# Low parts of the first weight pieces ordered behind the powers of the first norm, and reciprocals of row sums on 16 columns between two turns by 32x32 blocks

## The chip, the cores and the metric

The kernel runs on one core of a Trainium2 chip. The metric is the device time of one execution in microseconds (us), as the median of several runs. A core has five instruction queues that run beside each other and meet through semaphores: TensorE (PE in the rows, with its weight loads as PEld), VectorE (DVE), ScalarE (ACT), GpSimd (POOL) and SyncE (SP), from which the transfers (DMA) of this kernel are issued.

## The reference

One sequence of 512 tokens with 1024 channels goes through two blocks. The first block has three branches on one normed input, which are gated and merged; the second runs twice and has two attentions and an MLP.

```python
def rms_norm(x, g):
    y = xf * lax.rsqrt(jnp.mean(xf * xf, axis=-1, keepdims=True) + EPS)
    return (y * g).astype(x.dtype)

def first_block(...):
    h = rms_norm(x, g_norm)
    q, k, v, fl, gf, u, gs, qm, gm, gl = split_cols(h @ w_in)
    log_f = log_sigmoid(fl + b_forget)
    y_fox = forgetting_attention(q, k, v, log_f) * silu(gf)   # 12 heads of 64, causal softmax
    y_s5 = gelu(s5_ssm(u, ...))                               # diagonal complex scan
    y_s5 = y_s5 * sigmoid(y_s5 @ w_glu + b_glu) * silu(gs)
    y_mem = memory_attention(qm, mk, mv) * silu(gm)           # 4 heads, 256 memory tokens
    merged = sum of sigmoid(gl + b_merge) * (y_branch @ w_proj_branch)
    return rms_norm(x + merged @ w_out, g_final)

def second_block(x, c, ...):
    for l in range(2):
        h = rms(x, g_mix[l]) * (1 + sc1) + sh1                # sh, sc, gt from silu(c) @ w_ada
        y_a = gqa_attention(...) @ w_branch_a[l]              # 8 query heads, 2 key heads
        y_b = dilated_attention(...) @ w_branch_b[l]          # 3 groups of 4 heads, joined by their sums
        x = x + gt1 * ((gate_a * y_a + gate_b * y_b) @ w_out[l])
        x = x + gt2 * (square(relu(h2 @ w_ff1[l])) @ w_ff2[l])
```

Each softmax divides by the sum of its row; the change touches how the kernel forms the reciprocal of these sums, and the order of the work in the first `rms_norm`.

## The kernel before

**Layout and products.** Activations lie with channels on the 128 partitions and the 512 tokens along the columns. A float32 product is made of three matmuls on parts: each operand is split into a high part (rounded to fp32r) and a low part (the value less its high part), and PE adds high by high, high by low and low by high. Weights come in pieces of 512 KB by DMA into three buffers `wr`. `split` (L81) makes two tiles of each: the high part `wh` by a cast on ACT (L93), the low part `wl` by a subtraction (L96), on POOL for every second piece (`WP = 2`) and on DVE for the others. `get` (L105) hands out a piece; `ahead` splits the next three and fetches three more. For activations the high part is L229 or L231 on ACT (`h`), the low part L237 or L239 on DVE (`l`).

**The first norm.** It is done in two halves of 256 tokens. For one half, ACT squares each 128 channels (L186 for the first, L190 for the others, into `sq`), DVE adds them up (L191, `sacc`), PE sums over the partitions (L197, `ps`), DVE turns the sums into mean plus epsilon (L215, `nv`), POOL raises it to the power −0.5 (L217, `nr`), PE spreads the result over the partitions (L204), DVE multiplies x with it and the gain (L568, `hu`), ACT and DVE split it, and PE runs the first products: L600 and L601 take the high part of the activations with both parts of the weights, L606 the low part. In `head`, `stat(0)` and `stat(1)` issue the first half's and the second half's chain up to the spread. With `begun` false, which holds for the first block alone, `head` takes its three pieces by `get` between `stat(0)` and the first products, and calls `ahead` for the next three after the first half's high products (L603).

**The softmax units.** A unit covers two heads. DVE takes row maxima (L352, `unm`), PE forms scores (L327, `ps`), ACT exponentiates (L395, `pe`) and casts (L397, `ph`), DVE forms the low part (L399, `pl`), and PE multiplies with the values, to which columns of ones are joined, so that the product holds the row sums beside the output (L416 to L418, `ppv`). `out_item` ends a head: ACT copies the 64 rows of sums to one half of `rs` (L443) and the output to one half of `y` (L444). Every one of the 64 rows holds the same sum for its token. After the second head of a pair, DVE takes the reciprocal of the whole `rs` (L446), and POOL multiplies (L447). This happens 18 times: 6 in the first block and 6 in each layer of the second.

**What sets the order.** All tiles of 512 columns come from one ring of 73 buffers. The order of the instructions on each engine is found when the program is built, by a scheduler that plays a timeline of its own; a dependency of the kind `AFTER` holds in this order alone and leaves no wait in the program. The S5 branch is issued in small steps between the attention's items (`tick`): its scans (`s5g`, L1324), its mixed weights (`s5bw`) and, later, its low parts `yl` (L1128). In the second block keys and queries are normed and split in L652 to L726 (`xg`, `qk`, `kl`), and powers of small tiles are carried to PE through bfloat16 parts (L274 to L284, `mcq`).

Of the kernel before, what the change touches and what calls it, by code (L numbers as in the profile page):

```python
# [9 lines left out]
F32 = mybir.dt.float32  # L10
# [4 lines left out]
ALU = mybir.AluOpType  # L15
# [8 lines left out]
def f32(t):  # L24
    return t.bitcast(F32)


class Core:
    def __init__(self, ctx, tc, a):
        self.ctx, self.tc, self.nc, self.a = ctx, tc, tc.nc, a  # L30
        self.n = 0
        self.base = ctx.enter_context(tc.tile_pool(name="base", bufs=1))
        self.psx = ExitStack()
        self.psum({"mm": 3, "s": 4, "=a": "s", "pv": 1, "=m": "s"})
        self.wp = ctx.enter_context(tc.tile_pool(name="wp", bufs=1))
        self.ring = ctx.enter_context(tc.tile_pool(name="ring", bufs=1))
        self.strips = []
        self.iw = 0
        self.raw, self.hl, self.cur = {}, {}, {}
        self.bg = []  # L40
        self.sums = {}
        self.pe = None

    AFTER = mybir.DependencyInfo(mybir.DependencyClass.NoSync, mybir.DependencyReason.SCHED_ONLY)
    NU = 73
# [35 lines left out]
    def split(self, i):  # L81
        if i >= len(self.strips) or i in self.hl:
            return
        self.fetch(i)
        n = self.strips[i][1].shape[-1]
        r = self.raw.pop(i)
        self.raw[i] = None
        eng = self.nc.gpsimd if i % self.WP == self.WP - 1 else self.nc.vector
        self.hl[i] = []
        for c in range(0, n, T):  # L90
            m = min(T, n - c)
            h, l = self.u(F32R, "wh"), self.u(F32R, "wl")
            ins = self.nc.scalar.copy(h[:, 0:m], r[:, c:c + m])  # L93
            if self.pe is not None:
                self.tc.add_manual_dep(ins.ins, self.pe, self.AFTER, reason="weights")
            eng.tensor_tensor(out=l[:, 0:m], in0=r[:, c:c + m], in1=f32(h)[:, 0:m], op=ALU.subtract)  # L96
            self.hl[i].append((h, l))

    def ahead(self, i):
# [108 lines left out]
    def rstd(self, sacc, cols):  # L208

        nc = self.nc  # L210
        nb = len(cols)
        pq = self.p("m")
        self.sumcols(pq, sacc, cols)
        v = self.t(self.base, [128, 4], F32, "nv", 2)[:, 0:nb]
        nc.vector.tensor_scalar(out=v, in0=pq[:, 0:nb], scalar1=1.0 / D, scalar2=1e-6, op0=ALU.mult, op1=ALU.add)  # L215
        r = self.t(self.base, [128, 4], F32, "nr", 2)[:, 0:nb]
        nc.gpsimd.tensor_tensor(out=r, in0=v, in1=self.mhalf[:, 0:nb], op=ALU.pow)  # L217
        return self.bcast(r)

    def hsplit(self, src, bias=None, out=None):  # L220
# [6 lines left out]
    def hi(self, src, bias, out):  # L227
        if bias is None:
            self.nc.scalar.copy(out[0], src)  # L229
        else:  # L230
            self.nc.scalar.activation(out=out[0], in_=src, func=AF.Identity, bias=bias)  # L231

    def lo(self, src, bias, out):
        nc = self.nc
        h, l = out
        if bias is None:
            nc.vector.tensor_tensor(out=l, in0=src, in1=f32(h), op=ALU.subtract)  # L237
        else:
            nc.vector.scalar_tensor_tensor(out=l, in0=src, scalar=bias, in1=f32(h), op0=ALU.add, op1=ALU.subtract)  # L239


class Att(Core):
# [44 lines left out]
    def rows(self, mc, tag, psum_tag, out=None):  # L287

        nc = self.nc
        pt = self.turn(mc, psum_tag)  # L290
        if out is None:
            out = self.t(self.base, [128, T], BF16, tag, 2)
            nc.scalar.copy(out, pt)
        else:
            nc.scalar.copy(out[96:128], pt[96:128])
        return out

    def unit(self, nh, sregs, tregs, qk, vsl, dst, extra=None, nq=4, hd=64, orow=None, fold=None):

# [4 lines left out]
        nc = self.nc  # L304
# [99 lines left out]
        def pv_item(j, i):  # L404
            ph, pl, pvs = st.pop(("p", j, i))
            pv = st["pv", j]
            mm = nc.tensor.matmul
            for x, (g, kb, c) in enumerate(pvs):
                vh, vl = vsl(j, g, kb)
                o = c  # L410
                f = i == 0 and x == 0
                z = i == nt - 1 and x == len(pvs) - 1
                if not isinstance(c, slice):
                    o = slice(0, 4 * (c[1] - c[0]))
                h, lo = self.like(ph[:, o], c), self.like(pl[:, o], c)
                mm(self.cut(pv, c), vh, h, start=f, stop=False)  # L416
                mm(self.cut(pv, c), vl, h, start=False, stop=False)  # L417
                mm(self.cut(pv, c), vh, lo, start=False, stop=z)  # L418
            if i == nt - 1:
                out_item(j)  # L420

        def vrow(j):

            if own_sum:
                return slice(0, 128)
            o = 64 * (j % 2) if orow is None else orow(j)
            return slice(o, o + 64)

        def out_item(j):
            pv = st.pop(("pv", j))  # L430
            v = vrow(j)
            if own_sum:
                rb = self.u(name="rb")
                pb = self.p("m")
                nc.tensor.matmul(pb, self.selr1[j], st["mr"], start=True, stop=True)
                nc.scalar.copy(rb, pb)
                nc.vector.tensor_tensor(out=dst(j), in0=pv, in1=rb, op=ALU.mult)
                return
            if j % 2 == 0:
                st["rs"] = self.u(name="rs")  # L440
            rows = slice(64 * (j % 2), 64 * (j % 2) + 64)
            rs, y = st["rs"], dst(j)
            nc.scalar.copy(rs[rows], pv[64 - v.start:128 - v.start])  # L443
            nc.scalar.copy(y[rows], pv[v])  # L444
            if j % 2 == 1:
                nc.vector.reciprocal(out=rs, in_=rs)  # L446
                nc.gpsimd.tensor_tensor(out=y, in0=y, in1=rs, op=ALU.mult)  # L447

        s = [(lambda j=j, q=q: s_item(j, q)) for j in range(nh) for q in range(nq)]
# [35 lines left out]
class Blk2(Att):  # L485
# [93 lines left out]
    def head(self, names, h, posts, norm, view, byw=False, begun=False):  # L579

        pms = [self.p("mm" if i else "pv") for i in range(len(names))]
        stat, hi, lo = norm
        if not begun:
            stat(0)
        ws = [self.get(n, 8, begun) for n in names]
        if not begun:
            hi(0)
        stat(1)
        lo(0)
        for hf in range(2):  # L590
            if hf == 1:
                hi(1)
                lo(1)
            ah, al = [[view(t, hf) for t in ts] for ts in h]
            mm = self.nc.tensor.matmul
            wo = list(zip(ws, (view(pm, hf) for pm in pms)))
            for g in [[v] for v in wo] if byw else [wo]:
                for k in range(8):
                    for w, o in g:
                        mm(o, w[k][0], ah[k], start=k == 0, stop=False)  # L600
                        self.pe = mm(o, w[k][1], ah[k], start=False, stop=False).ins.name  # L601
                if hf == 0 and not begun:
                    self.ahead(self.iw)  # L603
                for k in range(8):
                    for w, o in g:
                        self.pe = mm(o, w[k][0], al[k], start=False, stop=k == 7).ins.name  # L606
        for pm, post in zip(pms, posts):
            self.done(pm, post)
            self.tick()
# [1511 lines left out]
```

## Time and profile before

| what | value |
|---|---|
| median of 3 runs | 2417.26 us (2416.67 to 2422.07) |
| the profiled execution's own time | 2420.52 us |
| its span in the trace | 2418.5 us |
| mean granted TensorE clock | 0.984 |
| TensorE busy | 2310.7 us, 96% |
| VectorE busy | 1508.5 us, 62% |
| ScalarE busy | 1055.8 us, 44% |
| GpSimd busy | 875.4 us, 36% |
| reciprocals of `rs` (L446) | 18, 60.2 us |

The page is made from one execution. Its span runs from the first to the last instruction in the trace; the execution's own time has some 2 us around it. A busy share is an average over the whole span. An engine's instruction has a start, a duration and, where the engine stood idle before it, the length of that idle time and what ended it. The chain that ended last is followed back from the end, each step to what released it.

### The profile page before, as it was taken

Reading aid. Unit: us, or ns where it says so; the run is one execution under the profiler, and the core shown is the slowest. Engines: PE = TensorE matmul, PEld = TensorE weight load, DVE = VectorE, ACT = ScalarE, POOL = GpSimd, SP = SyncE. Lnnn points to the kernel's source line nnn. Section 1 sums busy time; section 2 is a strip of 40 time slices with the busy share of each in tenths; the row PEclk is TensorE's granted clock in tenths of the full one; section 3 lists DMA queues with packets and bytes.
Section 4 is the critical chain, followed back from the end, with each engine's and each line's share of the span. In section 5 each row is a group of like instructions: output and inputs, shape, how many; then the busy total and the mean of one; then the engine's idle time right before and its main releaser. Section 6 shows DMA issues by size and latency. Waiting matters only on the chain.

```text
span 2418.5 us, 32948 instructions
## 1 busy us (share of the span) xinstructions
PE 2310.7 (96%) x12071; PEld 1933.5 (80%) x12098; DVE 1508.5 (62%) x2467; ACT 1055.8 (44%) x1973; POOL 875.4 (36%) x722
## 2 busy tenths in 40 slices
PE   6999999998999899999999999999899999999999
PEld 5877777877788877788888888888778888888888
DVE  6666778666899788657378673257864746422222
ACT  4354553453333436653444324334565433523432
POOL 2443556733232284235132223126521713222212
PEclk9999999999999999999999999999999999999999
DMA  5211122313576331122247563242211314223322
GB/s 171 78 44 53 44 84 95 118 49 115 207 258 247 117 107 52 53 83 85 68 132 260 199 219 122 79 140 75 79 44 51 116 53 140 75 94 111 100 84 87
DMA packets 105617, 265.37 MB, mean 110 GB/s; under 512 B 13664, under 2 KB 23408, under 8 KB 105456
## 3 DMA queue, kind: packets, MB, share of 16 engines
q1 hardware_dynamic: 104304, 261.50, 32.2%
q8 instruction: 95, 1.56, 0.3%
q10 hardware_dynamic: 1152, 1.77, 0.2%
q14 instruction: 66, 0.54, 0.1%
HBM read 244.72 MB, written 9.44 MB: 105 GB/s over the span
## 4 chain that ended last, share of the span: by engine, by line
PE 75%; DVE 11%; issue 5%; POOL 4%; ACT 3%; DMA 2%; SPq 0%; ACTq 0%; another core or an unknown queue 0%; POOLq 0%; DVEq 0%
PE pmm L124 19%; PE pmm L126 19%; PE pmm L125 19%; PE ps L327 5%; PE ppv L416 1%; PE ppv L418 1%; PE pmm L141 1%; PE ppv L417 1%; PE pmm L142 1%; PE pmm L140 1%; DVE wl L96 1%; DVE l L239 1%; ACT wh L93 1%; POOL wl L96 1%; DVE adacc L521 1%
## 5 line engine op out<-in xcount | busy, mean ns | idle before, releaser
L96 POOL TENSOR_TENSOR wl<-wr,wh 128x512 fp32r<-128x512 f32 x346 | 489.6, 1434 | 1160.3 <-ACT wh L93 1037.2
L126 PE MATMUL pmm<-h,wl 128*128 128x512 f32 (+1 forms) x2104 | 823.4, 392 | 9.0 <-POOL wl L96 5.3
L124 PE MATMUL pmm<-h,wh 128*128 128x512 f32 (+1 forms) x2104 | 823.3, 392 | 7.2 <-ACT wh L93 4.3
L125 PE MATMUL pmm<-l,wh 128*128 128x512 f32 (+1 forms) x2104 | 819.7, 390 | 0.0
L126 PEld LDWEIGHTS pmm<-h,wl 128*128 128x128 f32 x2104 | 399.6, 190 | 94.3 <-POOL wl L96 7.7
L124 PEld LDWEIGHTS pmm<-h,wh 128*128 128x128 f32 x2104 | 399.8, 190 | 86.2 <-ACT wh L93 5.6
L125 PEld LDWEIGHTS pmm<-l,wh 128*128 128x128 f32 x2104 | 399.6, 190 | 78.4 <-DVE l L237 0.8
L93 ACT CAST wh<-wr 128x512 fp32r<-128x512 f32 (+1 forms) x692 | 387.5, 612 | 146.3 <-DMA wr<-in_w 85.9
L96 DVE TENSOR_TENSOR wl<-wr,wh 128x512 fp32r<-128x512 f32 x346 | 276.2, 827 | 39.3 <-ACT wh L93 34.6
L399 DVE TENSOR_TENSOR pl<-pe,ph 128x512 fp32r<-128x512 f32 (+4 forms) x168 | 113.6, 689 | 132.1 <-ACT ph L397 131.1
L237 DVE TENSOR_TENSOR l<-r,h 128x512 fp32r<-128x512 f32 x64 | 46.6, 728 | 221.3 <-ACT h L229 216.5
L1010 DVE SCALAR_TENSOR_TENSOR x<-pmm,ada,x 128x512 f32<-128x512 f32 (+1 forms) x88 | 60.0, 682 | 178.7 <-PE pmm L126 178.3
L521 DVE SCALAR_TENSOR_TENSOR adacc<-adw,cact,adacc 128x512 f32<-128x512 f32 x168 | 154.4, 921 | 4.1 <-DMA adw<-in_wada 0.9
L327 PE MATMUL ps<-qk,qk 128*128 128x512 f32 (+4 forms) x416 | 140.8, 366 | 12.6 <-DVE unm L352 8.6
L1033 ACT ACTIVATE r<-pmm 128x512 f32<-128x512 f32 x62 | 37.1, 598 | 246.0 <-PE pmm L126 246.0
L395 ACT ACTIVATE pe<-ps 128x512 f32<-128x512 f32 (+4 forms) x168 | 84.5, 503 | 114.7 <-PE ps L327 113.3
L327 PEld LDWEIGHTS ps<-qk,qk 128*128 128x128 f32 x416 | 79.3, 192 | 29.4 <-DVE unm L352 12.4
L124 PE MATMUL pmm<-yh,wh 128*128 128x512 f32 (+1 forms) x244 | 90.4, 374 | 5.8 <-ACT yh L1466 3.8
L125 PE MATMUL pmm<-yl,wh 128*128 128x512 f32 (+1 forms) x244 | 90.4, 371 | 2.7 <-DVE yl L1128 2.7
L397 ACT CAST ph<-pe 128x512 fp32r<-128x512 f32 (+4 forms) x168 | 89.1, 530 | 6.5 <-ACT pe L395 0.4
L126 PE MATMUL pmm<-yh,wl 128*128 128x512 f32 (+1 forms) x244 | 89.5, 369 | 0.0
L352 DVE TENSOR_REDUCE unm<-ps 128x1 f32<-128x512 f32 (+2 forms) x112 | 65.1, 597 | 25.6 <-PE ps L327 25.3
(393 smaller groups left out, 3925.0 us busy)
## 6 DMA issues: line engine op xcount, KB each, us to landing
wr<-in_w SPq DMA_DIRECT2D x324, 512.0 KB
adw<-in_wada SPq DMA_DIRECT2D x192, 256.0 KB
xs<-xg SPq DMA_DIRECT2D x136, 64.0 KB
wr<-in_w SPq DMA_DIRECT2D x22, 384.0 KB
xd<-x SPq DMA_DIRECT2D x16, 256.0 KB
x<-xd SPq DMA_DIRECT2D x16, 256.0 KB
x<-in_x SPq DMA_DIRECT2D x16, 128.0 KB
x<-in_x SPq DMA_DIRECT2D x8, 256.0 KB
```

Source lines behind the costliest of these rows:

```text
L93: ins = self.nc.scalar.copy(h[:, 0:m], r[:, c:c + m])
L96: eng.tensor_tensor(out=l[:, 0:m], in0=r[:, c:c + m], in1=f32(h)[:, 0:m], op=ALU.subtract)
L124: mm(out, wh, ah, start=start, stop=False)
L125: mm(out, wh, al, start=False, stop=False)
L126: self.pe = mm(out, wl, ah, start=False, stop=stop).ins.name
L327: mm(outs[i] if len(r.shape) == 2 else outs[i].rearrange("p (r i) -> p r i", r=r.shape[1]), w, r, start=first and i == 0, stop=last and i ...
L352: nc.vector.tensor_reduce(out=nm, in_=pts[0], axis=AX.X, op=ALU.max, negate=True)
L395: nc.scalar.activation(out=e[:, w], in_=pt[:, w], func=AF.Exp)
L397: nc.scalar.copy(ph[:, w], e[:, w])
L399: nc.vector.tensor_tensor(out=pl[:, w], in0=e[:, w], in1=f32(ph)[:, w], op=ALU.subtract)
L521: nc.vector.scalar_tensor_tensor(out=acc, in0=w, scalar=cc, in1=acc, op0=ALU.mult, op1=ALU.add)
L1010: nc.vector.scalar_tensor_tensor(out=x[j][:, s], in0=pm[:, s], scalar=ada[:, c + j:c + j + 1], in1=x[j][:, s], op0=ALU.mult, op1=ALU.add)
```

## The change

There are two edits, independent of each other.

*The low parts of the first pieces.* `power` keeps the name of the last power instruction. In `head`, for the first norm alone, the low parts of its three pieces are ordered behind the first half's power, and those of the three pieces of `ahead` behind the second half's power, by the same kind of dependency, which holds in the order alone.

*The reciprocals.* `inv_rows` turns `rs` by blocks of 32x32 on DVE into a new ring tile `rt`, so that the 32 partitions of a block, all with the same sum for a token, become 32 equal columns and the tokens lie along partitions; takes the reciprocal of the first column of each of the 16 blocks (128x16); and turns it back, reading each of these columns 32 times.

```diff
--- before.py
+++ after.py
@@ -40,6 +40,7 @@
         self.bg = []
         self.sums = {}
         self.pe = None
+        self.lo_after = None
 
     AFTER = mybir.DependencyInfo(mybir.DependencyClass.NoSync, mybir.DependencyReason.SCHED_ONLY)
     NU = 73
@@ -93,7 +94,9 @@
             ins = self.nc.scalar.copy(h[:, 0:m], r[:, c:c + m])
             if self.pe is not None:
                 self.tc.add_manual_dep(ins.ins, self.pe, self.AFTER, reason="weights")
-            eng.tensor_tensor(out=l[:, 0:m], in0=r[:, c:c + m], in1=f32(h)[:, 0:m], op=ALU.subtract)
+            ins = eng.tensor_tensor(out=l[:, 0:m], in0=r[:, c:c + m], in1=f32(h)[:, 0:m], op=ALU.subtract)
+            if self.lo_after is not None:
+                self.tc.add_manual_dep(ins.ins, self.lo_after, self.AFTER, reason="behind the power")
             self.hl[i].append((h, l))
 
     def ahead(self, i):
@@ -214,7 +217,7 @@
         v = self.t(self.base, [128, 4], F32, "nv", 2)[:, 0:nb]
         nc.vector.tensor_scalar(out=v, in0=pq[:, 0:nb], scalar1=1.0 / D, scalar2=1e-6, op0=ALU.mult, op1=ALU.add)
         r = self.t(self.base, [128, 4], F32, "nr", 2)[:, 0:nb]
-        nc.gpsimd.tensor_tensor(out=r, in0=v, in1=self.mhalf[:, 0:nb], op=ALU.pow)
+        self.power = nc.gpsimd.tensor_tensor(out=r, in0=v, in1=self.mhalf[:, 0:nb], op=ALU.pow).ins.name
         return self.bcast(r)
 
     def hsplit(self, src, bias=None, out=None):
@@ -294,6 +297,16 @@
         else:
             nc.scalar.copy(out[96:128], pt[96:128])
         return out
+
+    def inv_rows(self, rs):
+
+
+        nc = self.nc
+        rt = self.u(name="rt")
+        nc.vector.transpose(out=rt, in_=rs)
+        ri = self.t(self.base, [128, 16], F32, "ri", 2)
+        nc.vector.reciprocal(out=ri, in_=rt.rearrange("p (b c) -> p b c", c=32)[:, :, 0])
+        nc.vector.transpose(out=rs.rearrange("p (b c) -> p b c", c=32), in_=ri.unsqueeze(2).to_broadcast([128, 16, 32]))
 
     def unit(self, nh, sregs, tregs, qk, vsl, dst, extra=None, nq=4, hd=64, orow=None, fold=None):
 
@@ -443,7 +456,7 @@
             nc.scalar.copy(rs[rows], pv[64 - v.start:128 - v.start])
             nc.scalar.copy(y[rows], pv[v])
             if j % 2 == 1:
-                nc.vector.reciprocal(out=rs, in_=rs)
+                self.inv_rows(rs)
                 nc.gpsimd.tensor_tensor(out=y, in0=y, in1=rs, op=ALU.mult)
 
         s = [(lambda j=j, q=q: s_item(j, q)) for j in range(nh) for q in range(nq)]
@@ -582,6 +595,7 @@
         stat, hi, lo = norm
         if not begun:
             stat(0)
+            self.lo_after = self.power
         ws = [self.get(n, 8, begun) for n in names]
         if not begun:
             hi(0)
@@ -600,7 +614,9 @@
                         mm(o, w[k][0], ah[k], start=k == 0, stop=False)
                         self.pe = mm(o, w[k][1], ah[k], start=False, stop=False).ins.name
                 if hf == 0 and not begun:
+                    self.lo_after = self.power
                     self.ahead(self.iw)
+                    self.lo_after = None
                 for k in range(8):
                     for w, o in g:
                         self.pe = mm(o, w[k][0], al[k], start=False, stop=k == 7).ins.name
```

The first place is POOL's order at the first norm. `nr_204` and `nr_290` are the powers of the two halves, `wl` the low parts; `wl_220` and `wl_224` belong to the second of the first three pieces, the other four to two of the next three. Before:

```order
L96 ISA
L96 TENSOR_TENSOR wl_220<-wr_145,wh_219 128x512
L96 TENSOR_TENSOR wl_224<-wr_145,wh_223 128x512
L217 TENSOR_TENSOR nr_204<-nv_202,mhalf_72 128x2
L96 TENSOR_TENSOR wl_352<-wr_217,wh_351 128x512
L96 TENSOR_TENSOR wl_356<-wr_217,wh_355 128x512
L96 TENSOR_TENSOR wl_368<-wr_237,wh_367 128x512
L96 TENSOR_TENSOR wl_372<-wr_237,wh_371 128x512
L217 TENSOR_TENSOR nr_290<-nv_288,mhalf_72 128x2
```

The same place after the change:

```order
L220 ISA
L220 TENSOR_TENSOR nr_204<-nv_202,mhalf_72 128x2
L97 TENSOR_TENSOR wl_220<-wr_145,wh_219 128x512
L97 TENSOR_TENSOR wl_224<-wr_145,wh_223 128x512
L220 TENSOR_TENSOR nr_290<-nv_288,mhalf_72 128x2
L97 TENSOR_TENSOR wl_352<-wr_217,wh_351 128x512
L97 TENSOR_TENSOR wl_356<-wr_217,wh_355 128x512
L97 TENSOR_TENSOR wl_368<-wr_237,wh_367 128x512
L97 TENSOR_TENSOR wl_372<-wr_237,wh_371 128x512
```

Each power has moved ahead of the low parts that stood before it. On DVE the first half's low parts stand behind `nv_202` in the same way, four of them still ahead of the first `hu`.

The second place is DVE's order in the second half, from the second of its squares' sums (`sacc_176`) to the first `hu`. Before:

```order
L191 TENSOR_TENSOR sacc_176<-sacc_176,sq_267 128x256
L191 TENSOR_TENSOR sacc_176<-sacc_176,sq_270 128x256
L191 TENSOR_TENSOR sacc_176<-sacc_176,sq_273 128x256
L96 TENSOR_TENSOR wl_360<-wr_227,wh_359 128x512
L191 TENSOR_TENSOR sacc_176<-sacc_176,sq_276 128x256
L96 TENSOR_TENSOR wl_364<-wr_227,wh_363 128x512
L191 TENSOR_TENSOR sacc_176<-sacc_176,sq_279 128x256
L191 TENSOR_TENSOR sacc_176<-sacc_176,sq_282 128x256
L215 TENSOR_SCALAR nv_288<-ps_285 128x2
L568 SCALAR_TENSOR_TENSOR hu_239<-x_127,cols_69,ps_292 128x256
```

After:

```order
L194 TENSOR_TENSOR sacc_176<-sacc_176,sq_267 128x256
L194 TENSOR_TENSOR sacc_176<-sacc_176,sq_270 128x256
L194 TENSOR_TENSOR sacc_176<-sacc_176,sq_273 128x256
L194 TENSOR_TENSOR sacc_176<-sacc_176,sq_276 128x256
L194 TENSOR_TENSOR sacc_176<-sacc_176,sq_279 128x256
L194 TENSOR_TENSOR sacc_176<-sacc_176,sq_282 128x256
L218 TENSOR_SCALAR nv_288<-ps_285 128x2
L97 TENSOR_TENSOR wl_360<-wr_227,wh_359 128x512
L581 SCALAR_TENSOR_TENSOR hu_239<-x_127,cols_69,ps_292 128x256
```

The two low parts have left the sums; one stands between the variance `nv` and `hu`, the other behind all eight `hu`.

The third place is DVE's order around the last reciprocal of the first block. `rs_3450` (`rs_3470` after) holds its sums, `yl` are low parts that PE waits for, `nv` belongs to the norm of the memory. Before:

```order
L1125 TENSOR_TENSOR s5du_3610<-s5du_3610,ps_3597 128x512
L1128 SCALAR_TENSOR_TENSOR yl_3731<-yf_1542,yh_3730 128x512
L1128 SCALAR_TENSOR_TENSOR yl_3736<-yf_1909,yh_3735 128x512
L215 TENSOR_SCALAR nv_3765<-ps_3760 128x2
L446 RECIPROCAL rs_3450<-rs_3450 128x512
L1128 SCALAR_TENSOR_TENSOR yl_3741<-yf_2348,yh_3740 128x512
L1128 SCALAR_TENSOR_TENSOR yl_3746<-yf_2694,yh_3745 128x512
```

After:

```order
L1141 TENSOR_TENSOR s5du_3630<-s5du_3630,ps_3617 128x512
L1138 TENSOR_SCALAR rd_3680<-ph_3679 128x512
L306 STREAM_TRANSPOSE rt_3694<-rs_3470 128x512
L218 TENSOR_SCALAR nv_3789<-ps_3784 128x2
L308 RECIPROCAL ri_3696<-rt_3694 128x16
L309 STREAM_TRANSPOSE rs_3470<-ri_3696 128x512
L1144 SCALAR_TENSOR_TENSOR yl_3755<-yf_1542,yh_3754 128x512
L1144 SCALAR_TENSOR_TENSOR yl_3760<-yf_1913,yh_3759 128x512
```

The two turns and the short reciprocal stand in the reciprocal's place, all ahead of the first `yl`, of which two stood ahead of the reciprocal before.

## Rows read from the trace of the kernel before

**Rows 1.** Page: busy us and share by engine; the chain that ended last

```profile
PE 2310.7 (96%) x12071; PEld 1933.5 (80%) x12098; DVE 1508.5 (62%) x2467; ACT 1055.8 (44%) x1973; POOL 875.4 (36%) x722
...
PE 75%; DVE 11%; issue 5%; POOL 4%; ACT 3%; DMA 2%; SPq 0%; ACTq 0%; another core or an unknown queue 0%; POOLq 0%; DVEq 0%
```

**Rows 2.** Waits of PE: line, waited for: us in total, times, longest

```profile
PE ps L197 <- DVE sacc L191: 14.9, 3, 11.9
```

**Rows 3.** Timeline, first half: start, us, operation, count [idle before <-releaser]

```profile
8.39 0.42 ACT L190 ACTIVATE sq<-x 128x256 f32<-128x256 f32 x1 [1.18 <-DMA x<-in_x]
...
11.44 0.42 DVE L191 TENSOR_TENSOR sacc<-sacc,sq 128x256 f32<-128x256 f32 x1
...
12.29 3.01 POOL L96 TENSOR_TENSOR wl<-wr,wh 128x512 fp32r<-128x512 f32 x2 [8.56 <-ACT wh L93]
...
13.49 2.36 DVE L96 TENSOR_TENSOR wl<-wr,wh 128x512 fp32r<-128x512 f32 x2 [0.37 <-ACT wh L93]
15.27 1.15 POOL L217 TENSOR_TENSOR nr<-nv,mhalf 128x2 f32<-128x2 f32 x1
...
17.73 3.23 DVE L568 SCALAR_TENSOR_TENSOR hu<-x,cols,ps 128x256 f32<-128x256 f32 x8 [1.88 <-PE ps L204]
...
18.71 0.58 PE L600 MATMUL ppv<-h,wh 128*128 128x256 f32 x1 [1.01 <-ACT h L229]
```

**Rows 4.** Timeline, second half of the first norm

```profile
23.89 3.30 DVE L191 TENSOR_TENSOR sacc<-sacc,sq 128x256 f32<-128x256 f32 x3
24.16 5.86 POOL L96 TENSOR_TENSOR wl<-wr,wh 128x512 fp32r<-128x512 f32 x4 [7.74 <-ACT wh L93]
...
27.11 1.77 DVE L96 TENSOR_TENSOR wl<-wr,wh 128x512 fp32r<-128x512 f32 x1
...
31.75 0.60 PE L197 MATMUL ps<-c,sacc 128*128 128x1 f32 x4 [2.52 <-DVE sacc L191]
...
32.63 0.71 POOL L217 TENSOR_TENSOR nr<-nv,mhalf 128x2 f32<-128x2 f32 x1 [2.61 <-DVE nv L215]
...
35.62 0.58 PE L600 MATMUL ppv<-h,wh 128*128 128x256 f32 x1 [1.01 <-ACT h L229]
```

**Rows 5.** Windows of 1 us, PE: busy (count), granted clock, DMA share, GB/s

```profile
38.00:39.00 1.00, 1.00 (x7) 0.50 0.00 0
39.00:40.00 1.00, 1.00 (x8) 0.75 0.00 0
```

**Rows 6.** Prices: the reciprocals' group (count, busy us, mean ns), single DVE rows

```profile
L446 DVE RECIPROCAL rs<-rs 128x512 f32<-128x512 f32 x18 | 60.2, 3344 | 18.7 <-ACT rs L443 18.7
...
504.21 0.25 DVE L375 RECIPROCAL uri<-usm 128x16 f32<-128x16 f32 x1 [1.41 <-ACT jk L349]
...
972.56 0.69 DVE L399 TENSOR_TENSOR pl<-pe,ph 128x512 fp32r<-128x512 f32 x1
...
106.45 0.43 DVE L1122 TENSOR_SCALAR rd<-ph 128x512 f32<-128x512 f32 x1
```

**Rows 7.** Timeline, reciprocals and the waits of PE behind them

```profile
317.01 3.32 DVE L446 RECIPROCAL rs<-rs 128x512 f32<-128x512 f32 x1
...
325.98 0.61 PE L418 MATMUL ppv<-pl,vh 128*128 128x512 f32 x1 [3.03 <-DVE pl L399]
...
361.06 3.33 DVE L446 RECIPROCAL rs<-rs 128x512 f32<-128x512 f32 x1
...
365.00 0.50 PE L125 MATMUL pmm<-yl,wh 128*128 128x512 f32 x1 [1.87 <-DVE yl L1128]
...
977.84 3.33 DVE L446 RECIPROCAL rs<-rs 128x512 f32<-128x512 f32 x1
...
983.63 0.50 PE L126 MATMUL pmm<-h,wl 128*128 128x512 f32 x1 [1.60 <-DVE wl L96]
...
1089.84 0.40 PE L284 MATMUL ps<-c,mcq 128*128 128x128 bf16 x4 [1.84 <-DVE mcq L278]
...
1787.29 0.50 PE L126 MATMUL pmm<-h,wl 128*128 128x512 f32 x1 [1.61 <-DVE wl L96]
```

## The prediction, made before the changed kernel ran

> **What bounds the kernel now.** I read the page's busy line and its chain first. TensorE (PE) is busy 2310.7 of 2418.5 us and holds 75% of the chain that ended last, VectorE (DVE) 11%, GpSimd (POOL) 4% [rows 1]. So an edit on DVE or POOL pays only where PE stands still, and PE stands still for 2418.5 − 2310.7 = 107.8 us in all. The view of PE's waits, read second, names what it stands for: the largest entry is the sums of squares, three waits of 14.9 us, 11.9 of them the one at the start of the program [rows 2]. The other two parts of the reading are stretches of the timeline: the two halves of the first norm [rows 3, 4], and the eighteen reciprocals with what PE does next [rows 7].
>
> **Part one, first half of the first norm.** The last square ends at 8.39 + 0.42 = 8.81, yet DVE adds it only at 11.44, since a low part of the weights stands ahead of it. Then POOL does two low parts, 12.29 to 15.30, before its power at 15.27, which ends at 16.42; hu follows at 17.73 and the first product at 18.71, 0.98 behind it [rows 3]. After the change the power stands ahead of both POOL low parts, and the add ahead of all of DVE's. What is late next: even with the add at its old end, 11.86, the power could start 0.94 later (in the second half, where nothing is ahead of it, it starts at 32.63, 0.88 after the sums at 31.75 that follow the last add at once), so at 12.80, end by 13.95 at its present 1.15, and hu would be allowed 1.31 later (17.73 − 16.42), at 15.26. But DVE still does the low parts ahead of hu, and its last two end at 13.49 + 2.36 = 15.85. Their casts on ScalarE (ACT) are where they were, so hu starts at 15.85 and not before: the gain is DVE's idle time ahead of hu, **1.88 us** [rows 3]. One thing speaks for less: ACT now squares the first piece of x's second half between two weight casts; if that piece is not there yet, ACT waits, and the nearest row for it is its 1.18 us wait for x at 8.39 [rows 3]. I take no such wait; the low end is 1.88 − 1.18 = 0.70.
>
> **Part one, second half.** PE starts the second sums at 31.75 after an idle 2.52 for the last add. Those adds cost 3.30 / 3 = 1.10 us each, beside POOL's four low parts (24.16 to 30.02) and behind DVE's own (1.77), against 0.42 for the one at 11.44 [rows 3, 4]. Afterwards POOL's four and DVE's low parts come behind the second power; six adds at 0.42 are done by 23.89 + 2.5 = 26.4, well before PE is free at 31.75 − 2.52 = 29.23. So the 2.52 us go. From the sums to the product the row stays 35.62 − 31.75 = 3.87, but for one thing: a DVE low part now stands right behind the variance and may run beside the power, which then takes the 1.15 us of the first half in place of 0.71 [rows 3, 4], 0.44 more. **2.52 − 0.44 = 2.08 us.** POOL's four low parts then run from about 31 to 37 beside the eight hu; those belong to later weight pieces, first used after this half's products, and their 5.86 us are covered by these. The half clock at the start of this half (granted 0.50 at 38 us, 0.75 in the next) remains: PE's gap shrinks, but doesn't close [rows 5]. The one transfer on SP that moves behind three small loads is a piece whose low part is no longer wanted before the power, so I cost it at nothing; without that cover it would cost the time of those loads. Part one in all: 1.88 + 2.08 = **3.96 us**, with ends 0.70 + 2.08 = 2.8 and 1.88 + 2.52 = 4.4.
>
> **Part two, the price of one.** A reciprocal of 128x512 takes 3.344 us, eighteen times, 60.2 in all. One of 128x16 takes 0.25, so it is paid by the column [rows 6]. In place of each come two turns and one of the short kind. No row shows a turn. The nearest rows for 128x512 are a one-input operation at 0.43 and a two-input one at 0.69 [rows 6]; beside a busy POOL such a row takes 1.77 [rows 4]. I take 0.69, the plain SBUF operation without a rival: the turn reads one input, but how fast it is for four-byte values is open, so I stay above 0.43. I add 0.07 for the seams, a guess on the safe side (the rows at 23.89 and 27.11 follow each other with none). So 2 x 0.69 + 0.25 + 0.07 = 1.70, a saving of **1.64** each; with 0.43 it is 2.16, with 1.77 a loss of 0.52. It breaks even at a turn of 1.51.
>
> The Trainium skill (VectorE: DVE Perf Modes, "Rules for kernel authors") advises fewer DVE operations rather than cheaper ones, since each pays its own drain; by that rule three in place of one would save nothing and the sum would be part one alone. The rows disagree here, for a reciprocal at least: 0.25 against 3.34 us.
>
> The same page ("The three transpose paths") gives 311 ns for a 128x128 turn of bf16; four of them, my estimate from that page, would be 1.24 us, the saving 0.54 each and the forecast by it 2411.1. No run here shows it.
>
> **Part two, where it reaches PE.** 18 x 1.64 = 29.5 us come free on DVE, but they count only where a reciprocal runs straight into an operation that PE waits for. Going along the eighteen, I find four [rows 7]. (a) At 317.01: three adds and the low part of a softmax follow without a gap, and PE waits 3.03 for it at 325.98. (b) At 361.06: the low parts yl follow, PE waits 1.87 at 365.00. (c) At 977.84: a low part of a key and one of a weight follow, PE waits 1.60 at 983.63. (d) The same in the second layer, 1.61 at 1787.29. In each the whole queue behind the reciprocal moves up by 1.64, capped by the wait: 1.64 + 1.64 + 1.60 + 1.61 = **6.49 us**. With turns of 0.43: 2.16 + 1.87 + 1.60 + 1.61 = 7.24. With turns of 1.77: a loss of 4 x 0.52 = 2.1. The planner also sorted anew what stands around (at 317 the turns come ahead of two groups of scans); since the same operations precede the adds, I cost that at nothing. If an operation that PE wants soon were pushed behind a turn, the price would be about one of them, 0.69. At the other fourteen DVE has slack before PE wants anything, or the wait ends on POOL or ACT as well; I count nothing.
>
> **Sum.** 3.96 + 6.49 = 10.45. Against the profiled execution's own 2420.52 us (span 2418.5 and 2.0 around it) that makes 2410.1; that execution lies 3.26 above the median 2417.26, inside the spread of the runs, so I take the sum from the median: **2406.8 us**.
>
> **Rivals.** *Only the norm pays.* The time set free on DVE falls into DVE's own next wait, because the operations that follow a reciprocal wait for ACT's casts or because the planner filled the place. For it: ACT is 44% busy and holds 3% of the chain [rows 1], and in all four places the low part needs a cast by ACT. Against: at the four places DVE runs without a gap from the reciprocal to the row that PE waits for. Time: 2417.3 − 4.0 = 2413.3.
>
> *More than that.* PE's gap before the second half becomes short enough that the clock stays at full: the stretch from 35.62, at 0.50 until 39 and at 0.75 in the next microsecond, costs 1.9 us (half of 3.4, and a quarter of one) [rows 4, 5]. And of two places where PE waits for a chain over DVE and POOL (1.84 at 1089.84 [rows 7], and its copy in the second layer) half goes, 1.8. With turns of 0.43 (0.75 more) it makes 4.45: 2402.4. Against: PE still stands still for at least the 3.87 from sums to product.
>
> *Slower.* A turn of four-byte values is slow, say as slow by the column as the reciprocal itself, 3.34. Then each place costs 2 x 3.34 + 0.25 + 0.07 − 3.34 = 3.66 more, and the four make 14.6 against part one's 3.96: 2417.3 + 10.7 = 2428.0. It takes back part one from 4 x (2t + 0.32 − 3.34) = 3.96, a turn of t = 2.0, and is told from no change from t = 2.6. Against: no SBUF row of this width but the reciprocal comes near that when nothing runs beside it [rows 6].
>
> *Not what it says.* The low parts are bound to the power only in the planner's order; the order of the changed program shows them behind it, so I give this no share of its own.
>
> **Numbers.** The forecast 0.52 (its own range 2402 to 2411), only the norm 0.19, more 0.18, slower 0.11. A measurement of this kernel can tell about 0.2%, 4.8 us, from no change, so faster means under 2412.4: forecast and "more", 0.70; within: "only the norm", 0.19; slower: 0.11. The range runs from 2398, below "more" by the spread of such estimates, to 2418, which holds "only the norm" and turns of up to about 1.9; it leaves out "slower" and a little below.
>
> **What would show it.** Right: the power ahead of both POOL low parts near 12.5, the first product near 16.8 in place of 18.71, the second sums with an idle of almost nothing, the second product 4.0 earlier; turns near 0.69; the four waits gone or shorter by 1.64. Wrong: hu still idle behind the broadcast, ACT waiting for x near 13, a low part of a weight late for the first products, turns of over 1.5, or the four waits there as before behind an ACT cast. The forecast falls if the first product of the second half is early but the end is not: then PE lost it again further on, and the view of its waits has a new line.

## The result, and the profile after

The changed kernel takes 2448.82 us (median of 4, 2448.14 to 2449.77) against 2419.2 for the kernel before on the same chip: a ratio of 1.0125, 95% interval 1.0112 to 1.0137. I had forecast 2406.8 and a range of 2398 to 2418. It is 30 us slower, and by a way that none of my cases described.

The page of the changed kernel, busy line and chain, answers to [rows 1]:

```profile
PE 2323.0 (95%) x12098; PEld 1945.4 (80%) x12098; DVE 1473.5 (60%) x2503; ACT 1054.3 (43%) x1973; POOL 865.1 (35%) x722
...
PE 76%; DVE 9%; issue 6%; ACT 4%; POOL 2%; DMA 2%; SPq 1%; POOLq 0%; ACTq 0%; DVEq 0%
```

The span grew by 2446.4 − 2418.5 = 27.9 us. PE's idle time (span less busy) went from 107.8 to 123.4, 15.6 more, and its busy time by 12.3 with the same products: that is the clock. Summed over 1 us windows (busy share times what is missing from a granted clock of 1.00), half-speed stretches cost 34.6 us before and 48.0 after, 13.4 more. DVE became 35 us less busy, as meant, and the kernel gained nothing by it.

The turns are as cheap as I took them. The groups of the three operations that stand for the reciprocal, of the changed kernel (count, busy us, mean ns, idle before), answer to [rows 6]:

```profile
L306 DVE STREAM_TRANSPOSE rt<-rs 128x512 f32<-128x512 f32 x18 | 12.8, 709 | 42.5 <-ACT rs L456 42.5
L309 DVE STREAM_TRANSPOSE rs<-ri 128x512 f32<-128x512 f32 x18 | 12.7, 707 | 0.5
L308 DVE RECIPROCAL ri<-rt 128x16 f32<-128x16 f32 x18 | 4.5, 248 | 0.5
```

0.709 + 0.707 + 0.248 = 1.66 us, where I had 1.70. The estimate of 1.24 us a turn that I made from the Trainium skill (VectorE: DVE Perf Modes, "The three transpose paths") was too high. The rule on fewer operations that I set against the change (the same page of the Trainium skill, "Rules for kernel authors") weighs their count against semaphores and says nothing of cheaper ones; here three operations of 1.66 us together took the place of one of 3.34.

The first norm of the changed kernel, from the timeline, answers to [rows 3, 4]:

```profile
8.57 0.42 DVE L194 TENSOR_TENSOR sacc<-sacc,sq 128x256 f32<-128x256 f32 x1 [0.37 <-ACT sq L193]
...
10.35 0.70 POOL L220 TENSOR_TENSOR nr<-nv,mhalf 128x2 f32<-128x2 f32 x1 [6.62 <-DVE nv L218]
...
13.58 0.42 ACT L189 ACTIVATE sacc<-x 128x256 f32<-128x256 f32 x1 [1.02 <-DMA x<-in_x]
...
15.06 1.94 DVE L97 TENSOR_TENSOR wl<-wr,wh 128x512 fp32r<-128x512 f32 x2 [2.46 <-DMA x<-in_x]
16.92 3.21 DVE L581 SCALAR_TENSOR_TENSOR hu<-x,cols,ps 128x256 f32<-128x256 f32 x8
...
17.88 0.58 PE L614 MATMUL ppv<-h,wh 128*128 128x256 f32 x1 [5.55 <-ACT h L232]
...
29.63 1.09 POOL L220 TENSOR_TENSOR nr<-nv,mhalf 128x2 f32<-128x2 f32 x1 [13.79 <-DVE nv L218]
...
32.50 0.39 PE L614 MATMUL ppv<-h,wh 128*128 128x256 f32 x1 [1.01 <-ACT h L232]
```

The power starts at 10.35 in place of 15.27, and the second half's first product stands at 32.50 in place of 35.62. So this part works, 3.1 us, and the lead is 3.3 at 70 us.

Where the time went, from the starts of the same matmuls in both timelines:

| before, us | after, us | after − before |
|---|---|---|
| 73.6 | 70.3 | −3.3 |
| 456.2 (behind the first block's 6 units) | 456.7 | +0.5 |
| 822.8 (among the first products of layer 1) | 823.4 | +0.6 |
| 1225.4 (behind the 6 units of layer 1) | 1242.3 | +16.9 |
| 1671.1 (among the first products of layer 2) | 1685.8 | +14.7 |
| 2055.4 (behind the 6 units of layer 2) | 2083.3 | +27.9 |

All of the loss lies where the 18 turns are; outside the attention stretches nothing is lost. Some of PE's waits have grown much. PE's waits before (line, waited for, us in total, times, longest):

```profile
PE ps L284 <- DVE mcq L278: 6.5, 5, 1.8
...
PE pmm L124 <- ACT wh L93: 5.7, 3, 3.6
...
PE pmm L124 <- ACT h L229: 2.4, 2, 1.2
```

And of the changed kernel:

```profile
PE pmm L127 <- ACT wh L94: 13.9, 8, 4.4
PE ps L287 <- DVE mcq L281: 13.8, 5, 5.1
...
PE pmm L127 <- ACT h L232: 9.5, 4, 3.6
```

PE waits longer for ACT's high parts of weights and of activations, though ACT does no more work than before. Together these two grew by 15.3 us (5.7 + 2.4 before, 13.9 + 9.5 after). The wait for `mcq`, which DVE makes and which is no tile of the ring, grew by 7.3.

One place shows how. It is the tenth reciprocal of the program. In the timeline before, ACT casts the next weights (`wh`) and the finished outputs (`h`) while the last head's product still runs; only then come the row sums and the reciprocal:

```profile
1030.90 1.14 ACT L93 CAST wh<-wr 128x512 fp32r<-128x512 f32 x2
...
1032.44 1.64 ACT L229 CAST h<-y 128x512 fp32r<-128x512 f32 x3
...
1035.82 0.58 ACT L443 COPY rs<-ppv 64x512 f32<-64x512 f32 x1 [1.73 <-PE ppv L418]
...
1036.43 3.35 DVE L446 RECIPROCAL rs<-rs 128x512 f32<-128x512 f32 x1 [1.45 <-ACT rs L443]
```

The same place of the changed kernel's timeline:

```profile
1042.75 0.58 ACT L456 COPY rs<-ppv 64x512 f32<-64x512 f32 x1 [4.33 <-PE ppv L431]
...
1043.36 0.71 DVE L306 STREAM_TRANSPOSE rt<-rs 128x512 f32<-128x512 f32 x1 [4.22 <-ACT rs L456]
1043.96 1.14 ACT L94 CAST wh<-wr 128x512 fp32r<-128x512 f32 x2
...
1045.61 1.65 ACT L232 CAST h<-y 128x512 fp32r<-128x512 f32 x3
...
1046.28 1.07 PE L127 MATMUL pmm<-h,wh 128*128 128x512 f32 x3 [3.56 <-ACT h L232]
```

ACT stood idle for 4.33 us ahead of the row sums, the time in which it made these casts before; now they all come behind the first turn, and PE waits 3.56 us for them. Windows of 1 us of PE just after it (length, busy, count, granted clock, DMA share, GB/s) show the second half of the price:

```profile
1046.00:1047.00 1.00, 0.72 (x3) 0.99 0.00 0
1047.00:1048.00 1.00, 0.35 (x2) 0.50 0.63 102
...
1052.00:1053.00 1.00, 1.00 (x4) 0.50 0.00 0
```

The clock falls to 0.50, the lower of its two levels, and stays there until 1053. By the same sum over windows the stretch costs about 3 us on top of the wait.

The two programs' orders say why the casts come late. `wh`, `h` and their low parts are tiles of the same ring as `rt`. I counted, for each of the 18 places, the ring tiles that the code asks for later than the row sums' result and that are nevertheless written first ahead of the reciprocal (or of the first turn):

```
before: 3 5 12 5 10 16 | 0 9 3 11 11 6 | 0 9 3 11 11 6     together 131
after:  0 0  0 0  0  0 | 0 0 0  0  0 0 | 0 0 0  0  0 0
```

In the changed kernel no later ring tile is written ahead of `rt`, at any place. The new tile is a gate. The rule behind it can be read in the programs too: in both, the first writes of all ring tiles (3362 before, 3380 after) stand in the order in which the code makes them, without one exception.

### The profile page after: what moved, and what is told of

It reads as the page before. It is cut to its first block, busy times and chain, and to the rows that moved or that the text cites. A ratio compares the mean times of both kernels' runs of the same rounds, so it can differ in the third digit from the quotient of the medians.

```text
span 2446.4 us, 33003 instructions
## 1 busy us (share of the span) xinstructions
PE 2323.0 (95%) x12098; PEld 1945.4 (80%) x12098; DVE 1473.5 (60%) x2503; ACT 1054.3 (43%) x1973; POOL 865.1 (35%) x722
## 3 DMA queue, kind: packets, MB, share of 16 engines
q10 hardware_dynamic: 1152, 1.77, 0.2%
## 4 chain that ended last, share of the span: by engine, by line
PE 76%; DVE 9%; issue 6%; ACT 4%; POOL 2%; DMA 2%; SPq 1%; POOLq 0%; ACTq 0%; DVEq 0%
PE pmm L129 20%; PE pmm L127 19%; PE pmm L128 19%; PE ps L340 5%; PE ppv L429 1%; PE ppv L431 1%; PE ppv L430 1%; PE pmm L144 1%; DMA xs<-xg 1%; DVE wl L97 1%; PE pmm L145 1%; PE pmm L143 1%; ACT wh L94 1%; POOL wl L97 1%; DVE l L242 1%
## 5 line engine op out<-in xcount | busy, mean ns | idle before, releaser
L97 POOL TENSOR_TENSOR wl<-wr,wh 128x512 fp32r<-128x512 f32 x346 | 479.3, 1404 | 1215.6 <-ACT wh L94 1090.1
L127 PE MATMUL pmm<-h,wh 128*128 128x512 f32 (+1 forms) x2104 | 826.5, 394 | 22.5 <-ACT wh L94 12.5
L365 DVE TENSOR_REDUCE unm<-ps 128x1 f32<-128x512 f32 (+2 forms) x112 | 65.2, 597 | 43.0 <-PE ps L340 42.6
```

The lines of the kernel that those rows point to most:

```text
L97: ins = eng.tensor_tensor(out=l[:, 0:m], in0=r[:, c:c + m], in1=f32(h)[:, 0:m], op=ALU.subtract)
L127: mm(out, wh, ah, start=start, stop=False)
L365: nc.vector.tensor_reduce(out=nm, in_=pts[0], axis=AX.X, op=ALU.max, negate=True)
```

## The experiments

**1 to 4: which part loses, and is it the operations or their order.** The first has the low parts behind the powers, with the old reciprocal:

```diff
-                self.inv_rows(rs)
+                nc.vector.reciprocal(out=rs, in_=rs)
```

> Only the low parts behind the powers; the old reciprocal of 128x512. The lead of the changed kernel before its first turn was 3.3 us, so both theories expect about 3.3 us less than before (ratio 0.9986). If this kernel is slower than before, the loss began in the norm.

Measured: ratio 0.9987 (0.9978 to 0.9997), 2416.57 us. The norm's part is a gain, and its size, 3.1 us, is near the 3.96 that I gave it.

The second has the turns alone, the two lines that set `lo_after` left out.

> Only the turns; the norm as before, the planner free. Both theories: about 33 us more than before (ratio 1.0135), since the changed kernel lost 28 us and had gained some 3 in the norm. If it is not slower, the two edits harm each other.

Measured: 1.0138 (1.0125 to 1.0152), 2453.57 us. The loss is in the turns, and the two edits don't harm each other.

For the third, the order of all five engines is given by a table of the kernel before's order, through dependencies that hold in the order alone and leave the choice of buffers to the planner; and the first turn writes in place, since with `rt` in the ring the old order can't be kept (the tiles behind it would stand ahead of it).

```diff
-        rt = self.u(name="rt")
-        nc.vector.transpose(out=rt, in_=rs)
+        nc.vector.transpose(out=rs, in_=rs)
...
         mixer_kernel(tc, out, **args)
+        pin_order(tc)
```

> The turns, with every engine's order held to that of the kernel before: the three new operations stand where the reciprocal stood, and the first turn writes in place, so that the ring of tiles is as before. Theory O (the loss is the new order that the planner found, and the turns themselves are cheap): 6.5 us less than before (ratio 0.9973), as forecast for the four places. Theory R (the turns themselves, or what they hold up on other engines, are dear): 20 us or more above before (1.008 and up).

Measured: 0.9996 (0.9986 to 1.0006), 2418.96 us. Not dear, so theory R falls; but the 6.5 us are not there either. Rows of its timeline show what became of the four places of [rows 7]:

```profile
321.34 0.50 PE L430 MATMUL ppv<-pl,vh 128*128 128x512 f32 x1 [1.40 <-DVE pl L411]
...
366.18 0.50 PE L128 MATMUL pmm<-yl,wh 128*128 128x512 f32 x1 [0.78 <-DVE yl L1140]
...
982.41 0.62 PE L339 MATMUL ps<-qk,qk 128*128 128x512 f32 x1 [2.27 <-DVE ut L368]
...
1787.79 0.50 PE L339 MATMUL ps<-qk,qk 128*128 128x512 f32 x1 [2.27 <-DVE ut L368]
```

Place (a) waits 1.40 in place of 3.03, 1.63 less, where a saving of 1.64 was forecast. Place (b)'s wait of 1.87 is gone (the row is the next one, 0.79 before). At (c) and (d) the waits for the weights' low parts are gone (1.60 and 1.61), but a product a little ahead of them now waits 2.27 each time, for a row maximum that stands behind those low parts on DVE. In the kernel before this product had no such wait. The table holds the order and not the buffers: of the 939 tiles that PE writes, 199 lie in another buffer here than before, and the scores of this product take one whose last reader is that row maximum, where before it was ACT. By the starts of the same matmuls PE falls back by 2.5 us against the kernel before at (c), and by 2.5 at (d). So this run is not the turns with all else equal. Its profile led by 7.7 us at 400 us and gave it back later, these 5.0 included; its half-speed stretches cost 42.6 us against 34.6, from windows as above. It is the profile of the slowest of the run's 11 executions (2425.45 us).

The fourth is the counterpart: the old reciprocal and no new tile, in the order that the planner found for the turns (by the same kind of table).

> The old reciprocal of 128x512, with every engine's order held to the one that the planner found for the turns. Theory O: as slow as the turns alone, and slower by what a reciprocal of 3.34 us in place of 1.67 costs on the path, 33 to 45 us above before (ratio 1.0135 to 1.0185). Theory R: within 5 us of before (0.998 to 1.002).

Measured: 1.0142 (1.0128 to 1.0155), 2454.38 us. The whole loss is there with this order, without a turn and without the new tile (20 later ring tiles are written ahead of the reciprocals, in place of 131); in it a reciprocal of 3.34 us costs no more, as far as the intervals tell, than the three operations of 1.66.

**5 to 7: whose order, and why it changed.** All three have the turns alone, the first one in place. In the fifth the table holds PE's order to the old one, in the sixth the other four engines' orders, in the seventh none.

> Turns only, the first turn in place; TensorE's order held to that of the kernel before, the other four engines' orders left to the planner. Theory P (TensorE's new order is what loses): within 5 us of before (0.998 to 1.002), as with all orders held. Theory Q (the order on the engines that feed it loses): 15 us or more above before (1.006 and up), near the turns alone at 1.0138.

Measured: 0.9958 (0.9943 to 0.9973), 2411.34 us: below both.

> The counterpart: VectorE, ScalarE, GpSimd and SyncE held to the order of before, TensorE's left to the planner, which knows the turns' costs. Theory P: 15 us or more above before (1.006 and up). Theory Q: within 5 us of before.

Measured: 1.0012 (1.0003 to 1.0022), 2422.24 us.

> Turns only, all orders free, but the first turn writes over the row sums, so that the ring of 73 tiles gives none away. If the extra tile in the ring is what upsets the order: within 5 us of before. If it is the new durations that the planner works with: 25 to 35 us above before (1.010 to 1.0145), as with the extra tile.

Measured: 0.9965 (0.9951 to 0.9978), 2411.87 us, better than the 5 us that I allowed. This one decides: with every order free and the same operations, the loss is gone as soon as the ring gives no tile away (125 later tiles are written ahead of the turns). My own guess, that the new durations upset the order, falls, and with it the question that 5 and 6 asked, because their first turn was in place and they had no loss to divide. What they do tell, with 3 and 7: the turns gain 0.35 to 0.42% where the engines that feed PE may be ordered anew (5, 7), and nothing where these are held (3, 6), though in 3 the two waits at (c) and (d) work against them.

**8: both parts, with the norm kernel's order held**, the turns in place.

> Both edits, with the order of the kernel that has the norm's edit alone, and the turns (in place) where its reciprocals stand. The sum of the two parts measured apart, 0.9987 and 0.9996: 0.9983, some 4 us below before. By my forecast for the turns it would be 10 us below (0.9957).

Measured: 0.9969 (0.9958 to 0.998), 2413.06 us. Between the two. That the held order keeps part of the gain away is likely, by experiment 10 below, but the intervals overlap.

**9 and 12: the gate by itself.** The ninth has no turn. Its only edit is the tile that the result goes to:

```diff
-                nc.vector.reciprocal(out=rs, in_=rs)
-                nc.gpsimd.tensor_tensor(out=y, in0=y, in1=rs, op=ALU.mult)
+                rt = self.u(name="rt")
+                nc.vector.reciprocal(out=rt, in_=rs)
+                nc.gpsimd.tensor_tensor(out=y, in0=y, in1=rt, op=ALU.mult)
```

> The old reciprocal of 128x512, no turn at all, but its result goes to a new tile of the ring, from which GpSimd multiplies. Theory G (the new ring tile is a gate: tiles of the ring are first written in the order in which the code asks for them, so no later tile, such as the next weights' parts, is written before the turn writes its own): 25 to 40 us above before (1.010 to 1.0165), though nothing is added but the tile's name. Rival D (the turns' durations or their reading pattern): within 5 us of before.

Measured: 1.0155 (1.0136 to 1.0173), 2457.1 us. In its program, too, no later ring tile is written ahead of the reciprocal at any of the 18 places. PE's waits have the same two lines from ACT as the changed kernel's:

```profile
PE pmm L124 <- ACT wh L93: 12.5, 8, 4.1
PE pmm L124 <- ACT h L229: 9.5, 4, 3.6
```

The twelfth has the turns and the ring tile, but opens the gate early:

```diff
                 st["rs"] = self.u(name="rs")
+                st["rt"] = self.u(name="rt")
+                nc.gpsimd.memset(st["rt"], 0.0)
...
-                self.inv_rows(rs)
+                self.inv_rows(rs, st["rt"])
```

> Turns only, into a tile of the ring as in the change, but the tile is asked for when the row sums' own tile is, and GpSimd clears it there (18 clears of 128x512 more), so that its first write doesn't wait for the sums. Theory G: the gate is open early, and the time is that of the turns in place, 0.995 to 0.999. If the extra tile costs by taking a buffer of the ring: 15 us or more above before.

Measured: 0.9939 (0.992 to 0.9957), 2404.54 us. 123 later tiles are again written ahead of the turns (131 before, 0 after the change). The tenth place in its timeline has the old order back, casts first, and no wait of PE behind it:

```profile
1018.38 1.14 ACT L94 CAST wh<-wr 128x512 fp32r<-128x512 f32 x2
...
1019.91 1.65 ACT L232 CAST h<-y 128x512 fp32r<-128x512 f32 x3
...
1023.55 0.58 ACT L457 COPY rs<-ppv 64x512 f32<-64x512 f32 x1 [2.00 <-PE ppv L430]
...
1024.23 0.71 DVE L305 STREAM_TRANSPOSE rt<-rs 128x512 f32<-128x512 f32 x1 [1.79 <-ACT rs L457]
```

and its waits of PE on ACT's `wh` and `h` are back at the old sizes, and that on `mcq` nearly:

```profile
PE ps L287 <- DVE mcq L281: 7.0, 4, 2.3
...
PE pmm L127 <- ACT wh L94: 5.7, 3, 3.6
...
PE pmm L127 <- ACT h L232: 2.4, 2, 1.2
```

So it is not the buffer that the tile takes from the ring, but the moment at which it is first written. The time is a little below the range that I gave and below that of experiment 7; the intervals of the two overlap, and why it should be faster was not tried.

**10 and 11: the change without the gate.** Both edits, the first turn in place, all orders free; and the same with PE's order held to the norm kernel's.

> Both edits of the change, all orders free, but the first turn writes over the row sums in place of a ring tile. Theory G: the two parts add, 0.9965 x 0.9987 = 0.9952, some 12 us below before. Rival D, or any harm that the two edits do each other: not below 0.9965.

Measured: 0.995 (0.9932 to 0.9967), 2407.67 us against 2418.64 for before. This is faster than both kernels, and the parts add as far as the interval tells.

> As the kernel with both edits in place, with TensorE's order held to that of the kernel with the norm's edit alone. If TensorE's old order suits the turns better, as the run with it held at 0.9958 against 0.9965 free may say: 0.9945, 13 us below before. If that difference was noise: the same as with the order free, 0.995.

Measured: 0.997 (0.9958 to 0.9982), 2412.36 us. Holding PE's order does not help here, so I take the difference between 5 and 7 for noise.

## Why the prediction was wrong

**The step that failed** is the sentence on the planner: it "sorted anew what stands around", and since the same operations precede the adds I cost that at nothing, or at one operation of 0.69 us if something were pushed behind a turn. It cost 41 us: the change takes 2448.82, and the same without the new tile 2407.67 (experiment 10). With the old reciprocal the new tile alone cost 38 (experiment 9). I looked at what stands ahead of each turn on DVE, and not at what on ACT and POOL now had to come behind it. `rt` was in the diff as one more tile of a ring of 73; I asked neither whether it could delay other tiles nor what its first write waits for. It waits for the last row sums of a pair of heads, the latest thing in a unit, while the ring's later tiles are the very weights and activations that PE wants next. The order was there to read: 131 first writes had left their place ahead of the reciprocals, two of the low parts `yl` at the third place of the change among them.

**The rivals.** I gave "slower" 0.11 and hung it on a turn of over 2.6 us. The side was right, the mechanism wrong: the turn took 0.71. "Only the norm pays" had 0.19; nothing speaks for it.

**The price of the turns** was right, 1.66 us for three operations against the forecast 1.70. **Their reach** was right in size and not in detail. Without the gate the turns alone give 0.9965, 8.5 us (5.3 to 11.9) where the sum had 6.49. But the four places are not the whole account: in the old order, where I had worked them out, (a) and (b) paid as forecast, (c) and (d) cost 2.5 us each in place of paying, by buffers chosen anew, and over the program nothing was left (0.9996). The gain of experiment 7 comes with an order, and with buffers, that the planner chose for the shorter operations; what of it is whose was not tried.

**The norm** was forecast at 3.96 us and gives 3.1 (0.9987; 0.7 to 5.3). The first half gained 0.83 rather than 1.88: ACT did wait for x, 1.02 us at 13.58, the bound that I had named and not taken, and DVE's last low part ended at 17.00 in place of 15.85. The second half gave 2.29 where I had 2.08 (35.62 to 32.50 is 3.12 in all): PE's idle of 2.52 ahead of the sums is gone, and the power took 1.09 beside DVE's low part, where I had 1.15.

**The sum.** The change without its gate takes 2407.67 us in a run where before takes 2418.64: 11 us less, where the forecast sum was 10.45. The two terms were sized about right, the turns' in part by luck, since it did not come as worked out for the four places; a third term, of the other sign and nearly four times their sum, was missing. A slip besides: by the sum, the range's end at 2418 holds turns of up to 2.1 us, not 1.9.

**Open.** Which of the gated tiles cost most was not tried. PE's idle time grew by 15.6 us net: the waits for `wh`, `h` and `mcq` grew by 22.6 together, and all else fell by 7.0. How the wait for `mcq` hangs on the gate was not followed; it came with it in experiment 9 (12.5) and all but went in experiment 12 (7.0). Why the turns in the held old order give nothing is shown in part: 5.0 us went at (c) and (d), and the half-speed stretches took 8 us more in its one profile.

## What to carry to other kernels

When tiles come from a shared ring and a planner lets no later tile be written ahead of an earlier one, a new tile is also a barrier: ask when it is first written, and which later tiles would have been written sooner. Write a late result over its input, or write its tile once early, as the clears of experiment 12 did. And where a change moves instructions, look in the order at what has come to stand behind the new operation on the other engines, above all on those that feed the engine that bounds. And an order that is held leaves the buffers free: experiment 3 kept every order and still had two waits that the kernel before had not.

## What the runs showed of the hardware that I had not expected

A turn of 128x512 float32 values by 32x32 blocks takes 0.703 to 0.709 us, and the way back, which reads 16 columns 32 times each, takes 0.706 to 0.712 (means of 18, in ten kernels): about what a two-input operation of that size takes (0.69, [rows 6]). No turn of the changed kernel took more than 0.712, though 15 of the 36 ran for more than half of their time beside an instruction of GpSimd, where the subtraction of [rows 4] took 1.77. And a wait costs PE more than its length: the 3.56 us at 1046.28 were followed by some 3 us lost at half clock, and over the program 15.6 us more of idle time came with 13.4 us more of lost clock.
